# Asking TensorE to keep its stationary operand in a prefix log-sum-exp kernel

## Chip, cores, metric

One core of a Trainium2 chip. The metric is the device time of one execution in microseconds. The median of the kernel before was 1262.91 us when the change was predicted.

## The reference

Input x is 4 x 4096 x 4128 in fp32. Along the second axis a running log-sum-exp is taken:

```python
out[:, 0, :] = x[:, 0, :].copy()
for t in range(1, S):
    mx = np.maximum(out[:, t - 1, :], x[:, t, :])
    out[:, t, :] = mx + np.log(np.exp(out[:, t - 1, :] - mx) + np.exp(x[:, t, :] - mx))
```

Every element is read once and written once: 541 MB in all.

## The kernel before

It works in 44 steps of up to 3 x 128 rows, and in each step on 4 chunks of about 1024 columns. ScalarE takes the exponential, TensorE sums along the rows with 128 x 128 matrices of zeros and ones, ScalarE takes the logarithm out of PSUM, and VectorE keeps the last row as the carry. There are four stationary operands: `incl` and `excl` (triangles), `ident`, and `pick` (brings in the carry). Cut to what matters:

```python
bufs = 4
def mm(pt, w, rhs, start=False, stop=False):
    nc.tensor.matmul(pt, lhsT=w, rhs=rhs, start=start, stop=stop, skip_group_check=True)
...
class Chunk:
    def head(self):                 # sums of a chunk's first row of three
        pt = self.pt = pmain.tile([P, CH], FP32, name="pt")      # CH = 1024, MM = 512
        for j in range(t.r):
            for s in range(0, CH, MM):
                mm(pt[:, s:s + MM], excl if j else incl, self.e(j, s, s + MM), start=j == 0)
        if not t.first:
            for s in range(0, CH, MM):
                mm(pt[:, s:s + MM], pick, carry[self.c][:, s:s + MM])
        if self.c == last:
            self.tail_head()        # the same for the last 32 columns, into qt
    def stage(self, j):             # one row: logarithm, then add the next row
        nc.scalar.activation(t.xt[:, j, c * CH:(c + 1) * CH], pt, ACT.Ln)
        if j + 1 < t.r:
            for s in range(0, CH, MM):
                mm(pt[:, s:s + MM], ident, self.e(j + 1, s, s + MM), stop=j + 2 == t.r)
            ...
        else:
            keep(carry[c], pt)
...
for g in range(len(chunks) + R - 1):
    for d in range(R - 1, -1, -1):
        if 0 <= g - d < len(chunks) and d < chunks[g - d].t.r:
            k = chunks[g - d]
            k.stage(d)
            if k.c == last and d + 1 == k.t.r:
                k.t.store()
                if stored + ahead < len(steps):     # ahead = bufs - 1
                    steps[stored + ahead].load()
                stored += 1
    if g + 2 < len(chunks):
        chunks[g + 2].exp()
    if g + 1 < len(chunks):
        chunks[g + 1].head()
```

The softmax here doesn't subtract the row's maximum and nothing guards it: scores larger than these inputs give would overflow.

Of the kernel before, what the change touches and what calls it, by code (L numbers as in the profile page):

```python
# [10 lines left out]
P = 128  # L11
R = 3
CH = 1024
# [4 lines left out]
def _constants(nc, pool):  # L18


    def tri(base, name):
        t = pool.tile([P, P], FP16, name=name)
        nc.gpsimd.memset(t, 1.0)

        nc.gpsimd.affine_select(  # L25
            out=t, in_=t, pattern=[[1, P]], compare_op=mybir.AluOpType.is_ge,
            fill=0.0, base=base, channel_multiplier=-1,
        )
        return t

    def ones_where_zero(bases, step, name):
        t = pool.tile([P, P], FP16, name=name)
        nc.gpsimd.memset(t, 0.0)
        for base in bases:
            nc.gpsimd.affine_select(  # L35
                out=t, in_=t, pattern=[[step, P]], compare_op=mybir.AluOpType.not_equal,
                fill=1.0, base=base, channel_multiplier=1,
            )
        return t

    return (
        tri(0, "incl"),
        tri(-1, "excl"),
        ones_where_zero([0], -1, "ident"),
        ones_where_zero([-(HI + 31), -(LO + 31)], 0, "pick"),
    )
# [3 lines left out]
def kernel(  # L50
# [11 lines left out]
    nc = tc.nc  # L62
# [3 lines left out]
    tail = D - n_main * CH  # L66
# [5 lines left out]
    incl, excl, ident, pick = _constants(nc, consts)  # L72
# [11 lines left out]

    ctx.enter_context(tc.manual_schedule())

    def mm(pt, w, rhs, start=False, stop=False):
        nc.tensor.matmul(pt, lhsT=w, rhs=rhs, start=start, stop=stop, skip_group_check=True)  # L88

    def keep(cr, pt):  # L90

# [26 lines left out]
    class Chunk:  # L118
# [13 lines left out]
        def head(self):  # L132
            t = self.t
            pt = self.pt = pmain.tile([P, CH], FP32, name="pt")
# [7 lines that stand above are left out]
                self.tail_head()  # L142

        def tail_head(self):


            t, r = self.t, self.t.r
            full = ptail.tile([P, R, tail], FP32, name="qt")
            qt = self.qt = full[:, :r, :]
            to = lambda v, n: v.unsqueeze(1).to_broadcast([P, n, tail])  # L150
            for i in range(r):
                e = self.e(i, CH, CH + tail)
                mm(qt[:, i:, :], incl, to(e, r - i), start=i == 0)
                if i:
                    mm(qt[:, :i, :], excl, to(e, i))
            if not t.first:
                mm(qt, pick, to(carry_t, r))

# [77 lines left out]
```

## Time and profile before

| | before |
|---|---|
| time, median | 1262.91 us |
| DMA, 100 to 1150 us | 433 GB/s |
| ScalarE busy | 947.3 us (75%) |
| TensorE matmuls | 688.7 us (55%), 2268 |
| weight loads | 237.0 us (19%), 2268 |
| granted TensorE clock | 0.771 |

In the lines of the profile below, PE stands for TensorE's matmuls, PEld for its weight loads, ACT for ScalarE, DVE for VectorE, POOL for GpSimd and SPq for the queue that issues the DMA transfers. The granted clock is the share of TensorE's full clock in the mean of the run. A transfer "lands" when its data have arrived.

Read the table from the second line: the DMA engines run all the time, and no compute engine does.

### The profile page before, as it was taken

What the parts mean: (1) busy time and instruction counts of PE and PEld (TensorE: products, weight loads), DVE (VectorE), ACT (ScalarE), POOL (GpSimd) and SP (SyncE); (2) the same over time, 40 slices, a digit from 0 to 9 for tenths busy, and PEclk for the clock granted to TensorE, in tenths of its full rate; (3) what the DMA queues carried; (4) which work ended last, traced back from release to release, by engine and by line L of the source; (5) the groups of instructions that cost most, each with busy time, mean ns of one, the idle gap of its engine ahead of it and who ended that gap; (6) DMA issues with size and microseconds to landing.
All of it is one profiled execution on the core that took longest, in us unless ns stands there. A gap on an engine that the chain in (4) does not pass through costs nothing.

```text
span 1261.0 us, 6165 instructions
## 1 busy us (share of the span) xinstructions
PE 688.7 (55%) x2268; PEld 237.0 (19%) x2268; DVE 451.4 (36%) x445; ACT 947.3 (75%) x733; POOL 2.2 (0%) x13
## 2 busy tenths in 40 slices
PE   3665554555555555655346555555634755664552
PEld 1222111111121111211112211111211211221120
DVE  2443333333333333334424333333442433333344
ACT  5997777777777777778569777777966977777794
POOL 0000000000000000000000000000000000000000
PEclk9887777777677777777768777787777777778786
DMA  9999999999999999999999999999999999999998
GB/s 411 410 439 431 432 427 434 438 430 432 433 437 431 432 432 436 432 427 436 431 433 436 437 429 431 436 436 432 430 434 435 432 431 432 434 435 431 433 422 347
DMA packets 12702, 541.46 MB, mean 429 GB/s; under 512 B 1408, under 2 KB 1408, under 8 KB 1408
## 3 DMA queue, kind: packets, MB, share of 16 engines
q1 hardware_dynamic: 12672, 541.07, 99.4%
q8 instruction: 18, 0.29, 0.1%
q14 instruction: 12, 0.10, 0.0%
HBM read 270.53 MB, written 270.53 MB: 429 GB/s over the span
## 4 chain that ended last, share of the span: by engine, by line
DMA 69%; ACT 21%; PE 5%; issue 2%; DVE 1%; SPq 0%; ACTq 0%
DMA xt<-in_x_dram 67%; ACT xt L128 11%; ACT xt L162 10%; PE pt L88 5%; DMA out_dram<-xt 2%; ACT xt L167 0%; SPq L116 0%; DVE carry L92 0%; DVE carry L93 0%; ACTq L231 0%; SPq L113 0%; ACTq L128 0%; PE qt L88 0%
## 5 line engine op out<-in xcount | busy, mean ns | idle before, releaser
L128 ACT ACTIVATE xt<-xt 128x3072 f16<-128x3072 f32 (+3 forms) x176 | 478.5, 2719 | 247.9 <-DMA xt<-in_x_dram 247.8
L88 PE MATMUL pt<-xt,ident 128*128 128x512 f16 x672 | 251.3, 470 | 530.7 <-ACT xt L162 530.4
L162 ACT ACTIVATE xt<-pt 128x1024 f32<-128x1024 f32 x512 | 487.6, 1030 | 2.5 <-PE pt L88 0.7
L92 DVE CAST carry<-pt 32x1024 f16<-32x1024 f32 x176 | 216.4, 1230 | 761.0 <-ACT xt L162 760.7
L88 PE MATMUL pt<-xt,excl 128*128 128x512 f16 x672 | 247.0, 504 | 0.0
L93 DVE TENSOR_TENSOR carry<-pt,carry 32x1024 f16<-32x1024 f32 x176 | 215.9, 1227 | 6.1
L88 PEld LDWEIGHTS <-ident 128*128 128x128 f16 x672 | 70.1, 104 | 677.7 <-issue 654.0
L88 PE MATMUL pt<-xt,incl 128*128 128x512 f16 x352 | 152.0, 526 | 23.6 <-ACT xt L128 15.0
L88 PEld LDWEIGHTS <-excl 128*128 128x128 f16 x756 | 92.5, 124 | 141.0 <-issue 108.1
L88 PE MATMUL pt<-carry,pick 128*128 128x512 f16 x320 | 109.8, 429 | 0.0
L88 PEld LDWEIGHTS <-incl 128*128 128x128 f16 x480 | 45.2, 111 | 129.7 <-DVE carry L93 95.2
L88 PEld LDWEIGHTS <-pick 128*128 128x128 f16 x360 | 40.6, 113 | 57.0 <-issue 34.3
L167 ACT ACTIVATE xt<-qt 128x96 f32<-128x96 f32 (+1 forms) x44 | 10.9, 249 | 45.7 <-PE pt L88 45.7
L92 DVE CAST carry_t<-qt 32x32 f16<-32x32 f32 x44 | 8.7, 197 | 25.5 <-ACT xt L167 25.4
L88 PE MATMUL qt<-xt,incl 128*128 128x64 f16 (+2 forms) x128 | 12.3, 196 | 0.0
L88 PE MATMUL qt<-xt,excl 128*128 128x64 f16 (+1 forms) x84 | 10.6, 187 | 0.0
L93 DVE TENSOR_TENSOR carry_t<-qt,carry_t 32x32 f16<-32x32 f32 x44 | 8.5, 193 | 1.5
L88 PE MATMUL qt<-carry_t,pick 128*128 128x96 f16 (+1 forms) x40 | 8.2, 204 | 0.0
L83 DVE MEMSET carry<- 128x512 uint32 x4 | 1.9, 485 | 1.1 <-PEq L220 1.0
L70 ACT ACT_TABLE_LOAD x1 | 1.3, 1283 | 0.8 <-PEq L220 0.8
L35 POOL TENSOR_SCALAR_AFFINE_SELECT pick<-pick 128x128 f16<-128x128 f16 x2 | 0.6, 294 | 0.1
L25 POOL TENSOR_SCALAR_AFFINE_SELECT incl<-incl 128x128 f16<-128x128 f16 x1 | 0.3, 294 | 0.0
(11 smaller groups left out, 1.9 us busy)
## 6 DMA issues: line engine op xcount, KB each, us to landing
xt<-in_x_dram SPq DMA_DIRECT2D x40, 6192.0 KB, 42.2
out_dram<-xt SPq DMA_DIRECT2D x40, 6192.0 KB, 28.1
xt<-in_x_dram SPq DMA_DIRECT2D x4, 4128.0 KB, 37.3
out_dram<-xt SPq DMA_DIRECT2D x4, 4128.0 KB, 23.0
```

Of the source, the lines that this page charges most:

```text
L25: nc.gpsimd.affine_select(out=t, in_=t, pattern=[[1, P]], compare_op=mybir.AluOpType.is_ge, fill=0.0, base=base, channel_multiplier=-1,)
L35: nc.gpsimd.affine_select(out=t, in_=t, pattern=[[step, P]], compare_op=mybir.AluOpType.not_equal, fill=1.0, base=base, channel_multiplier=1,)
L70: nc.scalar.preload_act_table_set("natural_log_exp_and_others")
L83: nc.vector.memset(t, 0.0)
L88: nc.tensor.matmul(pt, lhsT=w, rhs=rhs, start=start, stop=stop, skip_group_check=True)
L92: nc.vector.tensor_copy(cr[HI:HI + 32, :], pt[HI:HI + 32])
L93: nc.vector.tensor_tensor(out=cr[LO:LO + 32, :], in0=pt[HI:HI + 32], in1=cr[HI:HI + 32, :], op=mybir.AluOpType.subtract,)
L128: nc.scalar.activation(self.t.half[:, :, 2 * c0:2 * c0 + w], self.t.xt[:, :, c0:c0 + w], ACT.Exp,)
L162: nc.scalar.activation(t.xt[:, j, c * CH:(c + 1) * CH], pt, ACT.Ln)
L167: nc.scalar.activation(t.xt[:, :, t0:D], self.qt, ACT.Ln)
```

## The change

Intent: many matmuls in a row use the same stationary operand, and each brought its own weight load. The changed kernel remembers which operand was loaded last, and for a repeat it adds a matmul instruction of its own with `ldweights=False`. The small matmuls of the tail are regrouped, so that those with `incl` come first and those with `excl` after.

```diff
+    held = [None]
+
     def mm(pt, w, rhs, start=False, stop=False):
-        nc.tensor.matmul(pt, lhsT=w, rhs=rhs, start=start, stop=stop, skip_group_check=True)
+        if held[0] is not w:
+            nc.tensor.matmul(pt, lhsT=w, rhs=rhs, start=start, stop=stop, skip_group_check=True)
+            held[0] = w
+            return
+        pe = nc.tensor
+        pe.add_instruction(mybir.InstMatmult(
+            name=nc.get_next_instruction_name(),
+            ins=[pe.lower_ap(rhs), pe.lower_ap(w, for_matmul_weights=True)],
+            outs=[pe.lower_ap(pt, opt=True)],
+            start_tensor_calc=start, stop_tensor_calc=stop, ldweights=False,
+            tile_size=(P, P), tile_position=(0, 0), bass_skip_group_check=True,
+        ))
@@ tail_head
             for i in range(r):
-                e = self.e(i, CH, CH + tail)
-                mm(qt[:, i:, :], incl, to(e, r - i), start=i == 0)
-                if i:
-                    mm(qt[:, :i, :], excl, to(e, i))
+                mm(qt[:, i:, :], incl, to(self.e(i, CH, CH + tail), r - i), start=i == 0)
+            for i in range(1, r):
+                mm(qt[:, :i, :], excl, to(self.e(i, CH, CH + tail), i))
```

## The prediction

> **What bounds the kernel now.** I read the page's busy lines first, then its slice table, then the busy times of chosen windows, then the chain of waits and the timeline.
>
> ```profile
> PE 688.7 (55%) x2268; PEld 237.0 (19%) x2268; DVE 451.4 (36%) x445; ACT 947.3 (75%) x733; POOL 2.2 (0%) x13
> DMA  9999999999999999999999999999999999999998
> GB/s 411 410 439 431 432 427 434 438 430 432 433 437 431 432 432 436 432 427 436 431 433 436 437 429 431 436 436 432 430 434 435 432 431 432 434 435 431 433 422 347
> HBM read 270.53 MB, written 270.53 MB: 429 GB/s over the span
> ```
>
> No compute engine is above 75% (ScalarE). The DMA row is 9 in every slice but the last, and the rate is flat near 433 GB/s. The kernel reads and writes each element once, in fp32, so the bytes cannot shrink. 541.46 MB at 433 GB/s (the 100 to 1150 us window below) is 1250.5 us, against a span of 1261.0: only 10.5 us of the span is not paid for by bytes at the steady rate. These windows show where it lies (columns: window, its length, PE, PEld, DVE, ACT, POOL busy with counts, clock, DMA share, GB/s):
>
> ```profile
> 100.00:1150.00 1050.00, 580.80 (x1896) 199.18 (x1896) 372.69 (x366) 794.06 (x614) 0.00 (x0) 0.76 1.00 433
> ...
> 0.00:10.00 10.00, 0.00 (x0) 0.00 (x0) 1.97 (x5) 1.28 (x1) 2.17 (x13) 1.00 0.86 343
> 37.00:42.00 5.00, 2.67 (x12) 1.16 (x12) 2.46 (x2) 4.97 (x4) 0.00 (x0) 1.00 0.95 317
> ...
> 1227.00:1230.00 3.00, 0.65 (x3) 0.19 (x2) 0.90 (x1) 3.00 (x4) 0.00 (x0) 1.00 0.61 264
> 1230.00:1234.00 4.00, 3.64 (x10) 1.25 (x10) 1.92 (x3) 4.00 (x4) 0.00 (x0) 0.58 0.16 66
> 1258.00:1261.00 3.00, 0.00 (x0) 0.00 (x0) 0.00 (x0) 0.00 (x0) 0.00 (x0) 0.50 0.03 11
> ```
>
> Each window loses its length times (1 minus its rate over 433): start 2.1 us, the dip just before the first store takes effect 1.3 us, the gap at 1227 to 1234 us 1.2 + 3.4 = 4.6 us, the last landing 2.9 us. That is 10.9 us, the whole overhead within the scatter of short windows. Start and last landing hold no TensorE work. TensorE can touch only the dip at 37 us and the gap at 1227 us, 5.9 us together.
>
> Between those ends there is a backlog. In the chain of waits a load took this long from its issue to landing:
>
> ```profile
> 1107.99 2.76 ACT xt L128
> 1110.75 1.83 ACT xt L162 x2
> 1112.63 1.94 PE pt L88 x4
> 1114.84 2.65 ACT xt L128
> 1117.49 0.92 ACT xt L162
> 1118.44 1.24 DVE carry L92
> 1119.70 1.24 DVE carry L93
> 1120.98 3.25 PE pt L88 x8
> 1124.26 42.48 DMA xt<-in_x_dram
> ```
>
> The load is queued right behind a store, and the two are 12.38 MB, 28.6 us at 433 GB/s. So 42.5 - 28.6 = 13.9 us of older transfers were still queued when it was issued. The PE pieces in this chain (5% of the span by the page) are therefore not worth their length: compute that finishes earlier makes the queue longer and nothing else, and compute may be up to 13.9 us later before the DMA engines run dry.
>
> **What the Trainium skill says.** "DMA: Bandwidth & Descriptors", section "Where 436 GB/s comes from", gives 435.2 GB/s as the ceiling of the 16 ports. The trace agrees: 433 GB/s in the middle. "TensorE: Matmul & The Clock Gate" bears on the loads in two places that differ. Its "Step-by-step: what each phase is for" says that a weight load is pulled ahead of matmuls in flight if it goes to the background buffer; the list under "The mechanism" (packing) says that a load overlaps matmuls in flight only when its row group differs. All loads here use all 128 rows, and the timeline decides:
>
> ```profile
> 1220.41 0.74 PEld L88 LDWEIGHTS <-excl 128*128 128x128 f16 x4
> 1220.62 1.03 PE L88 MATMUL pt<-xt,excl 128*128 128x512 f16 x4
> ...
> 1232.18 0.15 PEld L88 LDWEIGHTS <-excl 128*128 128x128 f16 x1 [0.28 <-issue]
> 1232.57 2.87 ACT L162 ACTIVATE xt<-pt 128x1024 f32<-128x1024 f32 x3
> 1232.61 1.06 PE L88 MATMUL pt<-xt,excl 128*128 128x512 f16 x2
> 1232.61 0.15 PEld L88 LDWEIGHTS <-excl 128*128 128x128 f16 x1 [0.28 <-issue]
> ```
>
> At the full clock four matmuls with four loads take 1.03 us where two take 0.59 us in the same stretch, so one more costs 0.22 us. At half clock a load starts every 0.43 us, lasts 0.15 us and then idles 0.28 us. The page's section "Back-to-back issue gap" gives, for 512 columns with no load, 512/2.4 + 2.5 = 216 ns at full clock and 427 ns at half clock. The same section also gives 131 ns for a stream of load and matmul pairs, which this trace doesn't show. The matmuls with a load each already run at the pace of matmuls without one: the loads are hidden in both clock states.
>
> **The change, part by part.** *Loads removed.* The stationary operand changes once per group of ident, incl, excl, pick. There are 44 steps of 4 chunks, 4 steps without a carry. Loads left: ident 176; incl 176 + 44 tail = 220; excl 220, since the regrouped tail needs one instead of two in three-row steps; pick 160 + 40 = 200. Sum 816 of 2268, so 1452 go. At 237.0/2268 = 104.5 ns they are 152 us of weight-load busy time. All of it lies beside streaming matmuls, so TensorE's time to its last result falls by about 0 per wide matmul. Busy time of the weight loads should fall to 816 x 105 to 115 ns = 86 to 94 us (7%).
>
> *Tail regrouped.* The same 5 small matmuls and one pick per three-row step; their starts are already 0.03 us apart (1221.96 to 1222.08 holds five). Perhaps 0.03 us per step, under the backlog. *First store* (issued at 37.0 us): the chain from the second load's landing at 27.7 us holds one PE piece of 0.84 us, an ident pair at half clock. Its first load is prefetched and its second runs beside the first matmul: 0 to 0.05 us. *Gap at 1227 us*: it ends when the second-last store is issued at 1233.63. From the last landing (1220.7 us) to there ScalarE works nearly without a break; its one wait on PE is 0.68 us before the tail's Ln, an ident pair that starts 0.33 us after the preceding Ln and takes 0.59. The loads are again hidden: 0 to 0.1 us. After 1233.63 there are 10.32 MB, 23.8 us, plus landing, with no TensorE in it (the last store goes out at 1244.1 while the one before still moves). Sum: 0 to -0.2 us. From 1262.91 us I choose 1262.8.
>
> **The rivals.** (1) *The loads are exposed somewhere that I didn't see*, as the 19% might suggest. Even if TensorE cost nothing, no more than the 5.9 us can come back; I would expect at most 1.5 us, since ScalarE fills the gap at 1227: 1261.4. (2) *The clock falls*: fewer instructions could count as less activity, and the granted clock is already changing (mean 0.771). If every matmul ran at 427 ns, a step of 48 wide ones takes 20.5 us, under the 28.6 us of its transfers, and the backlog covers the lag. At the ends, the 10 to 12 matmuls in the path would take about 0.2 us more each, partly beside ScalarE: +0.5 to +1.5 us, so 1264. Against it: the array streams as long as before. (3) *A matmul without a load is slower*, if it waits for the one before to drain. A pair's 0.59 us less 0.22 of spacing leaves 0.37 us for one alone, so 0.15 us extra on each of 1452, 5 us per step: hidden by the backlog, and perhaps +1.5 us at the ends. Nothing in this profile speaks for it, and it can't be excluded as no such matmul is in it. (4) *Semaphores move*: the tail's Ln waits for ident matmuls that it doesn't read (45.7 us over 44 waits). New instructions could shift what it waits for, by up to 0.7 us either way at the end, nothing in the middle.
>
> **Range and chances.** Runs of before scatter 0.2 us. The ends can move about 1.5 us either way by clock phase and rivals 1 to 4, so 1261.0 to 1264.4. Faster by over 2% means under 1237.7 us: 541.46 MB would need 437.5 GB/s over the whole run, above the ceiling: 0.01. Slower by over 2% means over 1288.2 us: the step would have to outgrow its transfers, some three times the delay of rival 3: 0.01. Within 2%: 0.98.
>
> **What would show it.** Right: 816 weight loads, 2268 matmuls, weight-load busy near 90 us; groups of wide matmuls still 0.22 or 0.43 us apart; DMA near 433 GB/s from 100 to 1150 us; first store near 37 us, the gap near 1227 us of about the same size; the clock within some hundredths of 0.77. Wrong: wide matmuls without a load closer than 0.21 us would mean that the loads did cost; further apart, rival 3; a steady rate below 430 GB/s would mean that compute or a new wait has eaten the backlog, and my claim that the middle is immune falls.

## More of the kernel before

The page lists the queues of the DMA engines (packets, MB, share of 16 engines' span), and besides the data there is a queue that carries instructions:

```profile
q1 hardware_dynamic: 12672, 541.07, 99.4%
q8 instruction: 18, 0.29, 0.1%
q14 instruction: 12, 0.10, 0.0%
```

Queue 8 moves TensorE's program in pieces of 16 KB: 4536 instructions over 18 pieces are 252 in each.

## The result, and the profile after

The changed kernel took 1262.97 us in the median of 6 runs (1262.91 to 1263.89), the kernel before 1262.95 beside it (1262.84 to 1263.08). The ratio is 1.0002, interval 0.9989 to 1.0014. Here and below a ratio is the mean time of one kernel's runs over that of the other's of the same rounds, so it is not quite the ratio of the medians that are quoted.

The time is the predicted one. The page's busy line of the changed kernel shows that the way there is not:

```profile
PE 685.2 (54%) x2268; PEld 236.4 (19%) x2268; DVE 451.4 (36%) x445; ACT 947.3 (75%) x733; POOL 2.2 (0%) x13
```

There are still 2268 weight loads, where I had worked out 816. The groups say the same. Line 92 is the ordinary matmul, line 96 the instruction with `ldweights=False`, and that line, too, has a load for each of its matmuls (after the count: busy us, mean ns of one, then the idle time before them):

```profile
L92 PEld LDWEIGHTS <-excl 128*128 128x128 f16 x220 | 26.9, 122 | 36.7 <-issue 27.8
L96 PEld LDWEIGHTS <-excl 128*128 128x128 f16 x536 | 66.7, 124 | 103.4 <-issue 78.8
```

220 loads of `excl` at line 92 are the count that I had given for all that would stay. The other 536 should have gone.

The middle and the ends look as before: two windows of the changed kernel (same columns as in the prediction), and the same piece of the chain of waits.

```profile
100.00:1150.00 1050.00, 577.94 (x1896) 198.57 (x1896) 372.52 (x366) 793.90 (x614) 0.00 (x0) 0.76 1.00 433
1230.00:1234.00 4.00, 3.47 (x9) 1.13 (x9) 1.92 (x3) 4.00 (x5) 0.00 (x0) 0.62 0.16 66
1124.44 42.48 DMA xt<-in_x_dram
```

DMA still moves 433 GB/s, the gap before the second-last store is still there at 66 GB/s, and a load still takes 42.48 us from issue to landing. The first store went out at 37.26 us instead of 37.00.

The reason for the loads lies in the build, not on the chip. In the built program of the changed kernel each of the 2268 fp16 matmuls has a load instruction directly before it, and each of them, of both kinds, carries `ldweights=False`. The framework's lowering splits every fp16 matmul into a load and a matmul without one, and doesn't ask whether the kernel had set the flag. So the change asked for something that never reached the chip. What is left of it is the order of the tail.

### The profile page after: what moved, and what is told of

It is laid out like the page before. It is cut to its first block, busy times and chain, and to the rows that moved or that the text cites. A ratio compares the mean times of both kernels' runs of the same rounds, so it can differ in the third digit from the quotient of the medians.

```text
span 1261.2 us, 6165 instructions
## 1 busy us (share of the span) xinstructions
PE 685.2 (54%) x2268; PEld 236.4 (19%) x2268; DVE 451.4 (36%) x445; ACT 947.3 (75%) x733; POOL 2.2 (0%) x13
## 4 chain that ended last, share of the span: by engine, by line
DMA 69%; ACT 21%; PE 5%; issue 2%; DVE 1%; SPq 0%; ACTq 0%
DMA xt<-in_x_dram 67%; ACT xt L142 11%; ACT xt L175 10%; PE pt L96 3%; DMA out_dram<-xt 2%; PE pt L92 2%; ACT xt L180 0%; DVE carry L106 0%; DVE carry L107 0%; SPq L130 0%; ACTq L244 0%; SPq L127 0%; ACTq L142 0%; PE qt L92 0%
## 5 line engine op out<-in xcount | busy, mean ns | idle before, releaser
L142 ACT ACTIVATE xt<-xt 128x3072 f16<-128x3072 f32 (+3 forms) x176 | 478.3, 2718 | 247.9 <-DMA xt<-in_x_dram 247.8
L92 PE MATMUL pt<-xt,ident 128*128 128x512 f16 x176 | 77.5, 440 | 499.2 <-ACT xt L175 499.2
L96 PE MATMUL pt<-xt,ident 128*128 128x512 f16 x496 | 204.5, 480 | 35.0 <-ACT xt L175 34.7
L107 DVE TENSOR_TENSOR carry<-pt,carry 32x1024 f16<-32x1024 f32 x176 | 215.9, 1227 | 6.1
L96 PE MATMUL pt<-xt,excl 128*128 128x512 f16 x496 | 184.7, 490 | 0.0
L92 PE MATMUL pt<-xt,incl 128*128 128x512 f16 x176 | 92.4, 525 | 23.8 <-ACT xt L142 15.1
L96 PE MATMUL pt<-xt,incl 128*128 128x512 f16 x176 | 92.8, 527 | 0.0
L92 PE MATMUL pt<-xt,excl 128*128 128x512 f16 x176 | 92.5, 525 | 0.0
L92 PE MATMUL pt<-carry,pick 128*128 128x512 f16 x160 | 70.3, 440 | 0.0
L96 PE MATMUL pt<-carry,pick 128*128 128x512 f16 x160 | 66.4, 415 | 0.0
L180 ACT ACTIVATE xt<-qt 128x96 f32<-128x96 f32 (+1 forms) x44 | 10.9, 249 | 45.8 <-PE pt L96 45.8
L92 PEld LDWEIGHTS <-incl 128*128 128x128 f16 x220 | 22.9, 104 | 118.4 <-DVE carry L107 95.2
L96 PEld LDWEIGHTS <-incl 128*128 128x128 f16 x260 | 28.2, 117 | 11.7 <-issue 6.4
L92 PEld LDWEIGHTS <-pick 128*128 128x128 f16 x200 | 22.5, 112 | 29.1 <-issue 18.4
L96 PEld LDWEIGHTS <-pick 128*128 128x128 f16 x160 | 18.0, 113 | 27.0 <-issue 14.4
```

Source lines behind the costliest of these rows:

```text
L96: pe.add_instruction(mybir.InstMatmult(name=nc.get_next_instruction_name(), ins=[pe.lower_ap(rhs), pe.lower_ap(w, for_matmul_weights=True) ...
L107: nc.vector.tensor_tensor(out=cr[LO:LO + 32, :], in0=pt[HI:HI + 32], in1=cr[HI:HI + 32, :], op=mybir.AluOpType.subtract,)
L142: nc.scalar.activation(self.t.half[:, :, 2 * c0:2 * c0 + w], self.t.xt[:, :, c0:c0 + w], ACT.Exp,)
L180: nc.scalar.activation(t.xt[:, :, t0:D], self.qt, ACT.Ln)
```

## The experiments

Two questions: is that all that the change was; and what would it have been worth, had the loads gone? To take them out for real, the experiments called "loads out" edit the program after the framework has lowered it and before it is compiled. A load goes if it has the same operand as the load before it and takes part in no semaphore:

```diff
+def _drop_repeated_loads(nc):
+    for f in nc.m.functions:
+        for bb in f.blocks:
+            kept, held = [], None
+            for i in list(bb.instructions):
+                if i.opcode == "Ldweights":
+                    what, s = str(i.ins[0]), i.sync_info
+                    if what == held and (s is None or not (s.on_wait or s.on_update)):
+                        continue
+                    held = what
+                kept.append(i)
+            bb.instructions = kept
     with _tile.TileContext(nc) as tc:
         tile_prefix_logsumexp_kernel(tc, *args)
+    _drop_repeated_loads(nc)
```

All twelve kernels gave the right result.

### e1: the loads really out

The changed kernel with the edit above.

> The changed kernel with the 1452 repeated weight loads really taken out of the built program (the change's flag left all 2268 in the trace). Main theory (loads hidden behind streaming matmuls, and the DMA queue sets the end): 816 weight loads in the trace, weight-load busy 85 to 95 us, wide matmuls still 0.22 us apart at full clock and 0.43 us at half clock, steady DMA 433 GB/s, time 1262 to 1264 us, ratio 0.999 to 1.001. Rival A (loads exposed in the two places where TensorE sets when a store goes out): 1260.5 to 1262 us. Rival B (a matmul without its load waits for the drain of the one before): matmuls 0.37 us apart at full clock, time 1263.5 to 1265.

Measured: 1261.57 us (1261.46 to 1261.74, 5 runs), beside it before 1262.84 (1262.60 to 1263.10, 9 runs); ratio 0.9990, interval 0.9976 to 1.0004. The interval just reaches 1, but no run of one kernel lies among those of the other. Its busy line, then its timeline near 1219 us (start, length, engine, line, operation):

```profile
PE 682.4 (54%) x2268; PEld 85.9 (7%) x816; DVE 451.3 (36%) x445; ACT 947.2 (75%) x733; POOL 2.2 (0%) x13
```
```profile
1219.47 0.38 PE L92 MATMUL pt<-xt,excl 128*128 128x512 f16 x1
1219.69 0.81 PE L96 MATMUL pt<-xt,excl 128*128 128x512 f16 x3
1220.12 0.10 PEld L92 LDWEIGHTS <-pick 128*128 128x128 f16 x1 [0.77 <-issue]
1220.34 0.38 PE L92 MATMUL pt<-carry,pick 128*128 128x512 f16 x1
```

816 loads and 85.9 us: the count and the busy time that the prediction gave. Four matmuls, now without a load between them, start within 1220.34 - 1219.47 = 0.87 us, 0.217 us each. In the kernel before the same four with four loads lie between 1220.62 and 1221.49 us, again 0.87. So the loads were hidden. Yet 1.3 us are gone, and by which way was not clear: the time of rival A came out, but its place did not. The first store went out at 37.25 us, no earlier than before, and the last landing of a load was already 1.2 us early (1219.51 instead of 1220.69 us), before the gap at the end. The gain lies in the middle, where I had said that nothing could be gained.

One more line differs. The queue of TensorE's program in e1:

```profile
q8 instruction: 12, 0.20, 0.1%
```

1452 instructions less, 6 pieces of 16 KB less on the DMA engines, which are the bound. In the packed trace a piece holds one of the 16 engines for 1.0 us, while 15 packets of data run beside it. I call this theory F (fetches), against theory P (time of TensorE on the path of the stores).

### e2: the tail order alone

The kernel before with only the last hunk of the change.

> The kernel before with only the regrouped tail matmuls and every matmul in the ordinary form. Main theory (the flag changed nothing in the program that runs, the tail order is all that differs): the same stream of TensorE instructions as the changed kernel, 2268 loads, the same time within 0.1%, 1262.8 to 1263.3 us. Rival (the own instruction with its flag has some effect on the chip): another mean spacing, weight-load busy or idle than the changed kernel's 236.4 us and 685.2 us.

Measured: 1262.95 us (1262.76 to 1263.47, 5 runs), ratio to before 1.0001, interval 0.9989 to 1.0014; 2268 loads, 236.4 us. Its built TensorE program was compared with that of the changed kernel: 4536 instructions, all equal in operation, operands, flags and semaphores. So the changed kernel is this kernel, and the flag did nothing. That TensorE's matmuls were busy 689.3 us here and 685.2 there, with the same program, is the scatter of the granted clock (0.773 and 0.778).

### e3 and e4: TensorE as the bound, with and without repeated loads

Each head's matmuls are issued six times. Each pass starts the sum anew, so the result stays right:

```diff
+            for _ in range(6):
-            for j in range(t.r): ...
+                for j in range(t.r): ...
```

> The changed kernel with the matmuls of every chunk's head issued six times (each pass starts the sum anew, so the result stays right): TensorE becomes the bound. 6 x (352 + 672 + 320) + 672 = 8736 wide matmuls, 8988 loads. Main theory (a load is hidden behind a 512-column matmul): start-to-start 0.216 us at full clock, 8736 x 0.216 = 1887 us, time 1890 to 2000 us at a clock near full.

> The same with repeated loads taken out: 3376 loads left. Main theory: the same time as with loads, within 0.5%, since the array was streaming the whole time. Rival (a load in front of every matmul costs TensorE time that DMA hid in the changed kernel): faster by 5612 x 0.02 us = 110 us or more, over 5%.

Measured: 2074.52 us (2074.36 to 2075.01) with 8988 loads, 2074.72 us (2074.03 to 2074.90) with 3376; 4 runs each. The busy lines of e3 and e4:

```profile
PE 1923.9 (93%) x8988; PEld 862.2 (42%) x8988; DVE 451.4 (22%) x445; ACT 961.8 (46%) x733; POOL 2.2 (0%) x13
```
```profile
PE 1923.7 (93%) x8988; PEld 325.0 (16%) x3376; DVE 451.4 (22%) x445; ACT 961.8 (46%) x733; POOL 2.2 (0%) x13
```

537 us of load time went, and no time with it. Even where TensorE is the bound, a load in front of a 512-column matmul costs nothing. (My absolute time was low: 1887 us is the streaming alone, and at 93% busy TensorE also waits for ScalarE's logarithms.) DMA runs at 261 GB/s here, and 22 fetches more or less (70 and 48) don't show either.

### e5 and e6: narrow matmuls, with and without repeated loads

All matmuls but those of the first row are cut from 512 to 64 columns: 13916 matmuls.

```diff
+                MM = 64 if j else 512        # in head; 64 for pick and in stage
```

> The changed kernel with all matmuls but the first row's cut from 512 to 64 columns (13916 matmuls, a load each). If a load takes 0.03 us of the array's time or is hidden, starts are about 0.03 us apart and the time stays 1263 us; if a load holds up its matmul by its 0.10 us, a step's 312 narrow matmuls take 31 us, more than the 28.6 us of its transfers, and the time rises to 1400 us or more.

> The same with repeated loads taken out: 816 loads for 13916 matmuls. Starts about 0.03 us apart at full clock[...] and 0.053 at half; time 1260 to 1264 us. If narrow matmuls with a load each are slower than these, the loads' own rate is the cause and the flag's intent is worth something at this width; if not, loads are hidden even here.

Measured: 1294.58 us (1293.94 to 1294.84) with all loads, 1277.11 us (1276.98 to 1277.53) without the repeated ones; 4 runs each, before 1262.93 beside them. It looks as if loads cost 17.5 us at this width. The timeline of e5 at full clock, then that of e6:

```profile
704.42 0.97 PEld L96 LDWEIGHTS <-excl 128*128 128x128 f16 x31
704.45 1.07 PE L96 MATMUL pt<-xt,excl 128*128 128x64 f16 x31
```
```profile
706.67 1.07 PE L96 MATMUL pt<-xt,excl 128*128 128x64 f16 x31
```

31 narrow matmuls take 1.07 us with a load each, and 1.07 us without. Loads are hidden even here, TensorE is equally fast, and still both kernels are slower than with wide matmuls. My expectation for e6 (1260 to 1264 us) failed, and for e5 neither of the two times came (1263, or 1400 and more); with them fails any reading by TensorE's time. The instruction queues of e5 and e6:

```profile
q8 instruction: 109, 1.79, 0.5%
```
```profile
q8 instruction: 57, 0.93, 0.3%
```

91 and 39 fetches more than before, 31.65 and 14.18 us more: 0.35 and 0.36 us for each. The DMA rate from 100 to 1100 us is 424 and 430 GB/s, and ScalarE waits longer for loads (325.8 and 308.8 us in all, 247.8 before; the increase is about the time lost plus the 45.7 us by which the tail's Ln waited for PE before and no longer does). For PE, ScalarE waits 3.2 us in all in e5 and 4.6 in e6.

### e7 and e8: instructions on an idle engine, first try

If the fetches are the cause, instructions of an engine for which nobody waits must cost as well. Memsets of one partition on GpSimd, added to e1 (e7) and to the kernel before (e8):

```diff
+    idle = cpool.tile([P, 800], FP16, name="idle")      # e8: 96
...
+        for _ in range(9):                               # e8: 52, per chunk
+            nc.gpsimd.memset(idle[0:1, :], 0.0)
```

> The kernel with 816 loads, and 1584 memsets of one partition on GpSimd, which nobody waits for, spread over the run: instructions come back, but on an engine that is idle. Theory F (the 1.3 us that taking out loads gained are instruction fetches: 6 transfers of 16 KB less on the DMA engines, 12 instead of 18): about 6 fetches more on GpSimd's queue, time back near 1262.9, at least 1262.3 us. Theory P (they are time of TensorE on the path of the stores): 1261.4 to 1261.8 us as without the memsets.

> The kernel before with 9152 small memsets on GpSimd, about 36 fetches of 16 KB. Theory F, at the 0.2 to 0.36 us per fetch that the pairs before gave: 1262.9 + 7 to 13 = 1270 to 1276 us, with the DMA rate over the span under 429 GB/s and no engine later than DMA. Theory P: 1262.5 to 1263.5 us.

Measured: 1305.33 and 2088.31 us. Neither theory gave that: I had taken the memsets as too short, and GpSimd itself ended last (its memset pieces make up 94% and 79% of the chain). The times decide nothing. The stores, which GpSimd doesn't hold up, say a little: the last one was issued 1.70 us (e7) and 22.72 us (e8) later than in the kernel before, in e1 1.07 us earlier. The expectation of e11 starts from them. The repeat with shorter work is e11 and e12.

### e9: twice the head's matmuls

The loop of e3 with 2 in place of 6, in the kernel before: 3612 matmuls and loads.

> The kernel before with every head's matmuls issued twice (result right): 3612 matmuls and loads instead of 2268. My prediction's claim that the middle is immune to TensorE work up to the backlog, alone: 1262.5 to 1264 us. With theory F: 2688 instructions more, 10 or 11 fetches of 16 KB more, at 0.2 to 0.36 us each 2 to 4 us: 1265 to 1267 us. If TensorE itself became the path: over 1280 us with ScalarE waiting for PE.

Measured: 1266.65 us (1266.24 to 1267.17, 5 runs), ratio 1.0029, interval 1.0016 to 1.0041; 28 fetches, 10 more than before. The 3.6 us are inside theory F's range and outside my prediction's claim, but their place is not theory F's. The second store, and the PE piece of the chain of waits near 33 us, in the kernel before and then in e9:

```profile
63.44 0.34 SPq L116 DMA_DIRECT2D out_dram<-xt  x1
32.32 0.84 PE pt L88 x2
```
```profile
66.68 0.34 SPq L116 DMA_DIRECT2D out_dram<-xt  x1
33.73 5.75 PE pt L88 x18
```

The first store is 1.2 us late and the second 3.2 us, when either kernel has made one fetch of queue 8. Up to the second store the chain of e9 runs through the doubled matmuls. From there to the second-last store the lag stays between 1.8 and 4.8 us. So most of the 3.6 us is TensorE's time at the start, before there is a backlog, and e9 says little about fetches.

### e10: stores by chunk at the ends, loads out

A try at a version that beats both, which was to fill the dip at 37 us and the gap at 1227 us.

```diff
+    by_chunk = (steps[0], steps[-2], steps[-1])
...
+                if d + 1 == k.t.r and k.t in by_chunk:
+                    a, z = k.c * CH, D if k.c == last else (k.c + 1) * CH
+                    nc.sync.dma_start(out=k.t.dram(out)[:, :, a:z], in_=k.t.xt[:, :, a:z])
```

> A version to beat both: repeated loads out, and the first step and the last two stored chunk by chunk, so that the DMA engines have work in the dip at 37 us (1.3 us) and in the gap at 1227 to 1234 us (4.6 us). If these gaps are what the profile says, 1261.6 - 4 to 6 = 1255.5 to 1257.5 us; if the smaller pieces cost as much as they bring, 1260 us or more.

Measured: 1291.62 us (1291.43 to 1292.20, 4 runs), ratio 1.0227. Two lines of its waits (who waited for what: us in total, times, longest), and one of its chain:

```profile
ACT xt L142 <- DMA xt<-in_x_dram: 244.2, 41, 11.0
ACT xt L142 <- DMA out_dram<-xt: 42.5, 2, 24.4
```
```profile
1255.23 18.95 DMA out_dram<-xt
```

ScalarE's exponential, which writes other columns of the same tile, now waits for the landing of a store, 42.5 us in two waits. That wait doesn't exist in the kernel before. So the idea was not tested, it was blocked. A chunk would need a tile of its own. Whether the 4.6 us of the gap are to be had stays open.

### e11 and e12: instructions on an idle engine, shortened

As e7 with 560 columns, and as e8 with 20 memsets per chunk, so that GpSimd ends early.

> As e7 with shorter memsets (560 columns, about 0.55 us), so that GpSimd is done before the last store. About 13 instruction fetches of 8 KB more than without memsets. Theory F, at the 0.2 to 0.3 us per fetch by which the last stores of e7 and e8 went out late: 1261.6 + 2.6 to 4 = 1264.2 to 1265.6 us. Theory P (the 1.3 us were TensorE's): 1261.4 to 1261.8 us.

> As e8 with 3520 memsets, so that GpSimd is done near 800 us. About 27 fetches of 8 KB more. Theory F: 1262.9 + 5.5 to 8 = 1268.4 to 1271 us, TensorE, ScalarE and VectorE busy as before. Theory P: 1262.5 to 1263.5 us.

Measured: e11 1266.00 us (1264.57 to 1267.92, 5 runs, a wide scatter), e12 1277.03 us (1276.40 to 1277.13, 4 runs), beside 1262.97 of before. Theory P is out: TensorE, ScalarE and VectorE do the same work, and nobody waits for the memsets (the waits view puts 14.4 us of e12 down to them, in the first load of each of the four operands; these wait for GpSimd's constants, and 13.6 us of it pass before the first matmul). Theory F has the sign, but its size was too low, for e12 by half (14.1 us instead of 5.5 to 8). The queue line of e12, with 28 pieces of 8 KB more than before:

```profile
q14 instruction: 40, 0.33, 0.1%
```

When the time is lost is seen best on the stores' issues. First the kernel before, then e12, two stores each:

```profile
321.15 0.34 SPq L116 DMA_DIRECT2D out_dram<-xt  x1
780.75 0.34 SPq L116 DMA_DIRECT2D out_dram<-xt  x1
1212.01 32.45 SPq L116 DMA_DIRECT2D out_dram<-xt  x3
```
```profile
325.09 0.34 SPq L117 DMA_DIRECT2D out_dram<-xt  x1
794.92 0.34 SPq L117 DMA_DIRECT2D out_dram<-xt  x1
1226.34 32.27 SPq L117 DMA_DIRECT2D out_dram<-xt  x3
```

The lag is 3.9 us at the first pair, 14.2 at the second and 14.3 at the third. It grows while GpSimd still issues, and stops growing when GpSimd has run out, near 804 us.

Could it be the memsets and not their fetches, say by their writes to SBUF? GpSimd was busy 889.6 us in e11 and 599.2 in e12, and the shorter busy time lost more (14.1 us, against 4.3 us of e11 over e1, both taken as the distance to before). And e7, with the same 13 fetches as e11 and 1209.9 us of memsets, sent its last store 1.70 us late, e11 5.65. The loss goes with the number of fetches, 13 and 28, not with the memsets' time, and e5 and e6 have no memset at all. That argues for the fetches, but the number of memsets grows with theirs (1602 and 3560); the two were not separated by a run in which GpSimd's program is fetched but not executed.

All pairs together:

| kernel | fetches more or less | time more or less | per fetch |
|---|---|---|---|
| e1 against before | 6 less (16 KB) | 1.27 us less | 0.21 us |
| e9 against before | 10 more (16 KB) | 3.62 us more | not to be read: mostly TensorE's start |
| e6 against before | 39 more (16 KB) | 14.18 us more | 0.36 us |
| e5 against before | 91 more (16 KB) | 31.65 us more | 0.35 us |
| e11 against e1 | 13 more (8 KB) | 4.30 us more | 0.33 us |
| e12 against before | 28 more (8 KB) | 14.06 us more | 0.50 us |

## Why the prediction was right, and where it was not

*What bounds the kernel: right.* DMA sets the time, 433 GB/s before and after. TensorE's load time of 152 us was worth nothing by itself: e1 took it out and e4 took out 537 us under a TensorE bound.

*"The loads are hidden in both clock states": right,* and shown by e1, e3 and e4, and further than I had claimed: at 64 columns, too.

*"816 of 2268, so 1452 go": wrong for this kernel.* This is the step that failed. The count of groups was right (e1 has 816 loads and 85.9 us), but I took the flag at its word. None went. The predicted time came out because I had given the step no worth, and in part by luck: but for the tail's order, the program timed was the one before. The time alone could not show that it had failed; the count in the busy line did, and the prediction had named it as the thing to look at.

*"0 to -0.2 us" for loads that go: too small.* With the loads out the time falls by 1.3 us, 0.1%. That is the figure of rival 1 (1261.4), but not its way: nothing was exposed on TensorE.

*"Compute that finishes earlier makes the queue longer and nothing else", the middle as immune: wrong in one point.* The backlog does cover TensorE's time once it is there. It doesn't cover what the instructions themselves seem to put on the DMA engines. In e12 the engines that wait for data do the same work, and the lag of the stores grows through the middle, to 14.2 us; in e5 it grows to 29.1 us at the store that comes out at 1212.01 us in the kernel before. Instructions appear in two places, on their engine and in the DMA queue, and I looked only at the first.

*"TensorE can touch only the dip at 37 us and the gap at 1227 us": too narrow.* e9 lost 3.2 us up to the second store at 63.44 us, before the backlog had built up.

*"12.38 MB, 28.6 us", "13.9 us": a slip.* The page's KB are of 1024 bytes: a store and a load of 6192 KB are 12.68 MB, 29.3 us at 433 GB/s, and 13.2 us of older transfers were queued. The 10.32 MB and 23.8 us at the end are 10.57 MB and 24.4 us. The expectation of e5 repeats the 28.6 us. No conclusion hangs on it.

*Rivals 2 to 4* could not show in the change, as the loads stayed. In e1, where they went, the clock was 0.777 (0.771 before), the spacing 0.217 us, and the tail's Ln waited for PE as before (45.8 us over 44 waits, 45.7 before).

*What stays open:* why a fetch that holds one of 16 engines for 1.0 us costs 0.2 to 0.5 us of the whole and not a sixteenth. A transfer has landed when the last of its 16 parts has, so an uneven spread of the fetches would do that. The packed traces keep the landing of each part, though no view shows them, and they fit. In the median transfer the last part lands 4.2 to 5.0 us after the first in the three kernels with 18 pieces on queue 8 and no memsets (before, changed, e2), but 7.2 us after it in e12, 8.4 in e6 and 10.2 in e5. In e1 the first part of the last load lands at 1213.27 us (before 1213.39), the last part at 1219.51 (1220.69): the gain is almost all the last part's. Which engine carries the fetches was not seen, and a piece of queue 14 takes 0.31 us while e12 lost 0.50 for each, so the time on one engine is not the whole of it. Nor is the cost even: the figures per fetch are means. That e1's 1.3 us are fetches rests on the count, on these landings and on the other pairs; at 0.21 us each they lie at the lower edge. It is argued, not shown.

## What to carry to other kernels

Look for the instruction that a change removes, in the count of its group, before you read anything into the time: a number that is right can hide that the change never took place. Weight loads in front of matmuls were free on TensorE in every pair of runs here, at 512 columns and at 64. In a kernel that is bound by DMA, count instructions as bytes as well: here every 250 of TensorE's went with 0.2 to 0.4 us of time, and two kernels with more instructions on an idle engine were slower, too. And before a run is put down to a cause, see where in the run its time was lost: e9 had the time that theory F forecast, at a place that was TensorE's.

## What the Trainium skill lacked or had wrong

- "TensorE: Matmul & The Clock Gate", "The mechanism": its list of what overlaps says that loads overlap matmuls in flight only with another row group. Here all loads use all 128 rows and cost nothing: 2074.52 us with 8988 loads, 2074.72 us with 3376, and 1.07 us for 31 matmuls of 64 columns with or without a load each. Its other account ("Step-by-step: what each phase is for", background buffer) agrees.
- The same page, "Back-to-back issue gap": the sustained 131 ns for load and matmul pairs of 512 columns doesn't appear. The spacing was 217 ns with and without a load.
- "Runtime: NRT & Kernel Launch", "Instruction fetch mechanics", calls the cost of crossing a block of 16 KiB mostly hidden. In this kernel, which DMA bounds, the pairs of runs lost 0.21 to 0.36 us with each piece of 16 KB (1.0 us of one DMA engine) and 0.33 to 0.50 us with each of 8 KB; the cause is argued, not shown.
- No page that I found says that the framework's lowering puts a load in front of every fp16 matmul whatever `ldweights` says (2268 loads of 2268).
